# A mixing projection as seven products of quarters, with the second norm's operands through DRAM and three heads at the MLP's start

## The chip, the cores and the metric

The kernel runs on one core of one Trainium2 chip. The metric is the device time of one execution in microseconds (us); the median of three runs of the kernel before is 2449.32 us (2448.23 to 2449.37). The engines are TensorE (PE; its weight loads stand as PEld), VectorE (DVE), ScalarE (ACT), GpSimd (POOL) and SyncE (SP). POOL and SP issue the DMAs here, each from a queue of its own that works in order.

## The reference

One layer on 512 tokens of width 2048, float32 in and out. What matters here is the second half:

```python
conv_branch = jnp.einsum('bsc,cd->bsd', conv_y, w_conv_out[l])      # 1024 -> 2048
attn_branch = jnp.einsum('bsc,cd->bsd', attn, w_attn_out[l])        # 1024 -> 2048
merged = gc * conv_branch + ga * attn_branch
x = x + jnp.einsum('bsd,de->bse', merged, w_mix_out[l])             # 2048 -> 2048
h = rmsnorm(x, g_mlp[l])
u = jnp.square(jax.nn.relu(jnp.einsum('bsd,df->bsf', h, w_ff1[l]))) # 2048 -> 8192
x = x + jnp.einsum('bsf,fd->bsd', u, w_ff2[l])
return rmsnorm(x, g_final)
```

`gc` and `ga` are sigmoid gates. `rmsnorm` divides each row by the root of its mean square and multiplies by a gain per column.

## The kernel before

**Arithmetic.** Every float32 operand of a matmul is split into a high part in the matmul's format and the rest (`split`, L101 on ScalarE and L102 on VectorE), and each product is made of three matmuls: high times high, low times high, high times low.

**Seven products.** Most projections are made in groups of 512 output columns by a scheme of seven products of quarters instead of eight. Rows (256 tokens each) and columns (256 each) are halved, the inner dimension is halved into even and odd blocks of 128. The activations' quarters A11, A12, A21, A22 give seven operands: A11, A12, A22 themselves, S1 = A21 + A22, S3 = A11 - A21, S2 = S1 - A11, S4 = A12 - S2. The weights' quarters X[i, j] are loaded one by one (1 MB each, `Group.load`, on SP's queue, into four slots x0 to x3) and combined by VectorE in place (L105). `Group.head` makes the products A11 and A12 from X[0, 0] and X[1, 0]; `Group.tail` makes S4, S2, S3, S1 and A22, `Group.tail2` S1, S3, S2, S4 and A22 in that order. In `tail`, S4 takes X[1, 1] as it is, and S2 and S3 take differences with it. Each product is 48 matmuls of 256 columns. The banks that collect them are called a, b, c and d; ScalarE's snapshots (L207) and VectorE's additions (L108) combine them, and a `put` takes each finished quarter (i, j). The split halves th and tl have two buffers each. A `Group` may carry an extra matmul of 192 columns ahead of a product (L138) or beside it (L712).

**Order.** The program is traced in order and a planner then arranges each engine's instructions by their program order and by when it reckons them ready. A tile is named by its tag; a tag has the number of buffers given, most have one, and a new tile of a tag waits for the last use of the old one. Between PE's stages there is no barrier.

**The stages around the change.**

- `conv_out(c)` (L818): the conv projection for 512 columns as seven products of half size (24 matmuls each), with weights in three slots, two tiles per group. `put` (L832) multiplies by the gates and leaves the quarter in `held`, in slot x1; for c = 3 it goes to DRAM (`held_d`, L834). The gates come by POOL's queue (L824).
- `attn_out(c)`: the attention projection as an ordinary sum over eight blocks (`gemm_t`, L347 to L349, 96 matmuls of 512 columns). For each of four banks, VectorE multiplies by the gate (L847) and adds `held` (L108), and the sum is split into the operand M of the mixing (eight splits of 256 columns). The attention operands themselves stand in t3 and t2. The order is conv 0, attention 0, conv 1, attention 1, conv 2, conv 3, attention 2, attention 3.
- The mixing (`gemm_n`, L354 to L356): M is stationary, 512 weight columns move; 16 blocks of the inner dimension, four row tiles, four column blocks, three matmuls each. The weights come in 24 loads of 1 MB (L326), since column blocks 2 and 3 are passed over twice, for two row tiles each time. `add_into` adds x, sums squares on ScalarE (L380) and writes the new rows to DRAM (L898).
- The class `Blocks`: while later blocks of the mixing run, finished rows are transposed on TensorE (L935, 64 in all), multiplied by the gain (L943), and the seven operands of the MLP are made from them and stay in SBUF.
- The MLP's first half: 16 groups `ff1(g)` of 512 columns. Group 0 is `head(True, rest)`, `Q2.sums(3)` and `tail2`, where `rest` turns the last rows and computes the rows' factors; groups 1 to 15 are `head` and `tail`. `put_u` squares the quarters, makes the seven operands of the second half's left side (the two `sums`, L1041, L1057, L1058) and writes them to DRAM (L1060, L1061). Groups 1 to 15 carry the extra matmul beside S2 (L712). The fourth weight slot of group 0 is x1, which before it held rows of the mixing (`rows_block`).
- The MLP's second half follows and is not touched.

## Time and profile before

| what | value |
| --- | --- |
| median of three runs | 2449.32 us |
| profiled execution, first to last instruction | 2450.8 us (the profile gives no other time of it) |
| mean granted TensorE clock | 0.999 |
| TensorE busy / weight loads | 2423.2 us / 2252.6 us |
| VectorE, ScalarE, GpSimd busy | 1970.8, 1180.1, 230.3 us |
| first conv group starts, first mixing matmul, first MLP matmul | 864.75, 1031.4, 1211.8 us |
| second half of the MLP starts | 1830.2 us |

A row of a table of stretches gives the stretch, its length, and for each engine the busy us and the number of instructions (x), then the granted clock, the share of DMA time and GB/s. A row of the timeline gives start, duration, engine, line, operation, output <- inputs, and in brackets how long the engine was idle before and what ended that. A row of groups gives line, engine, operation, tiles, shapes, count, then busy us and mean ns of one, then idle time before and what ended it. Matmul ends are modelled and overlap: the time between starts tells the pace.

### The profile page before, as it was taken

Reading aid. Unit: us, or ns where it says so; the run is one execution under the profiler, and the core shown is the slowest. Engines: PE = TensorE matmul, PEld = TensorE weight load, DVE = VectorE, ACT = ScalarE, POOL = GpSimd, SP = SyncE. Lnnn points to the kernel's source line nnn. Section 1 sums busy time; section 2 is a strip of 40 time slices with the busy share of each in tenths; the row PEclk is TensorE's granted clock in tenths of the full one; section 3 lists DMA queues with packets and bytes.
Section 4 is the critical chain, followed back from the end, with each engine's and each line's share of the span. In section 5 each row is a group of like instructions: output and inputs, shape, how many; then the busy total and the mean of one; then the engine's idle time right before and its main releaser. Section 6 shows DMA issues by size and latency. Waiting matters only on the chain.

```text
span 2450.8 us, 40086 instructions
## 1 busy us (share of the span) xinstructions
PE 2423.2 (99%) x17224; PEld 2252.6 (92%) x17224; DVE 1970.8 (80%) x1665; ACT 1180.1 (48%) x1189; POOL 230.3 (9%) x369
## 2 busy tenths in 40 slices
PE   8999999999999999999999999999999999999998
PEld 8999899999999999888899999999998888888886
DVE  7987777788887777535688898888988888889898
ACT  6443434345455544335555666666655333333334
POOL 0100000111121110000000000000011001100000
PEclk9999999999999999999999999999999999999999
DMA  7664544454656654635645646656588566655662
GB/s 250 183 192 142 154 133 146 138 160 165 211 172 214 215 186 155 216 114 205 199 169 185 231 173 216 216 202 228 177 302 293 168 247 227 237 191 183 244 225 101
DMA packets 276597, 475.62 MB, mean 194 GB/s; under 512 B 10732, under 2 KB 180836, under 8 KB 276036
## 3 DMA queue, kind: packets, MB, share of 16 engines
q1 hardware_dynamic: 232592, 291.59, 37.0%
q0 software_dynamic: 42960, 180.38, 19.8%
q8 instruction: 135, 2.21, 0.4%
q10 hardware_dynamic: 868, 1.10, 0.1%
q14 instruction: 42, 0.34, 0.0%
HBM read 374.46 MB, written 98.57 MB: 193 GB/s over the span
## 4 chain that ended last, share of the span: by engine, by line
PE 93%; DVE 3%; DMA 1%; issue 1%; ACT 1%; POOL 0%; SPq 0%; DVEq 0%; POOLq 0%; ACTq 0%
PE a L145 6%; PE a L147 6%; PE a L149 6%; PE d L149 5%; PE d L145 5%; PE d L147 5%; PE a L163 5%; PE a L165 5%; PE a L162 5%; PE c L145 4%; PE c L147 4%; PE c L149 4%; PE b L145 3%; PE b L147 3%; PE b L149 3%; PE d L165 3%
## 5 line engine op out<-in xcount | busy, mean ns | idle before, releaser
L101 ACT ACTIVATE th<-x 128x2048 fp32r<-128x2048 f32 (+1 forms) x252 | 483.4, 1918 | 462.3 <-DVE x L105 153.8
L102 DVE TENSOR_TENSOR tl<-x,th 128x2048 fp32r<-128x2048 f32 (+1 forms) x252 | 575.1, 2287 | 159.0 <-ACT th L101 144.1
L105 DVE TENSOR_TENSOR x<-x,x 128x2048 f32<-128x2048 f32 (+1 forms) x144 | 329.2, 2286 | 19.9 <-DMA x<-in_w_in_dram 16.2
L101 ACT ACTIVATE th<-y 128x2048 fp32r<-128x2048 f32 (+1 forms) x109 | 184.8, 1700 | 268.8 <-PE a L163 138.8
L102 DVE TENSOR_TENSOR tl<-y,th 128x2048 fp32r<-128x2048 f32 (+1 forms) x109 | 218.9, 2013 | 30.0 <-ACT th L101 29.5
L162 PE MATMUL a<-th,us 128*128 128x512 f32 x512 | 199.2, 389 | 0.0
L163 PE MATMUL a<-th,us 128*128 128x512 f32 x512 | 199.2, 389 | 0.0
L145 PE MATMUL a<-ST,th 128*128 128x256 f32 x752 | 174.1, 277 | 0.6 <-ACT th L101 0.6
L147 PE MATMUL a<-ST,th 128*128 128x256 f32 x752 | 173.6, 277 | 0.0
L102 DVE TENSOR_TENSOR tl<-raw,th 128x2048 fp32r<-128x2048 f32 x32 | 73.4, 2292 | 101.8 <-ACT th L101 101.5
L145 PEld LDWEIGHTS a<-ST,th 128*128 128x128 f32 x752 | 141.3, 188 | 0.9 <-ACT th L101 0.8
L147 PEld LDWEIGHTS a<-ST,th 128*128 128x128 f32 x752 | 141.3, 188 | 0.0
L165 PE MATMUL a<-tl,us 128*128 128x512 f32 x512 | 136.8, 389 | 0.0
L145 PE MATMUL c<-S,th 128*128 128x256 f32 x576 | 134.2, 278 | 0.0
L147 PE MATMUL c<-S,th 128*128 128x256 f32 x576 | 133.8, 277 | 0.0
L101 ACT ACTIVATE th<-t 128x2048 fp32r<-128x2048 f32 x31 | 59.5, 1920 | 126.1 <-DVE t L105 73.0
L145 PE MATMUL d<-ST,th 128*128 128x256 f32 x512 | 118.2, 277 | 0.0
L147 PE MATMUL d<-ST,th 128*128 128x256 f32 x512 | 118.2, 277 | 0.0
L162 PEld LDWEIGHTS a<-th,us 128*128 128x128 f32 x512 | 96.1, 188 | 20.0
L165 PEld LDWEIGHTS a<-tl,us 128*128 128x128 f32 x512 | 96.0, 188 | 20.1 <-DVE tl L102 0.2
L163 PEld LDWEIGHTS a<-th,us 128*128 128x128 f32 x512 | 96.1, 188 | 19.9
L101 ACT ACTIVATE th<-raw 128x2048 fp32r<-128x2048 f32 x32 | 61.4, 1919 | 103.0 <-PE pn L356 42.7
(362 smaller groups left out, 6517.3 us busy)
## 6 DMA issues: line engine op xcount, KB each, us to landing
x<-in_w_in_dram SPq DMA_DIRECT2D x86, 1024.0 KB, 5.9
x<-in_w_ff_dram SPq DMA_DIRECT2D x64, 1024.0 KB, 8.4
y<-in_w_ff_dram SPq DMA_DIRECT2D x64, 1024.0 KB, 8.4
us<-s_d POOLq DMA_DIRECT2D x48, 1024.0 KB, 9.2
s_d<-rh POOLq DMA_DIRECT2D x32, 896.0 KB, 5.5
s_d<-r POOLq DMA_DIRECT2D x32, 896.0 KB, 5.5
raw<-in_w_mix_out_dram SPq DMA_DIRECT2D x24, 1024.0 KB, 5.2
g_d<-o POOLq DMA_DIRECT2D x32, 256.0 KB, 3.1
```

Of the source, the lines that this page charges most:

```text
L101: nc.scalar.activation(out=hi, in_=src, func=AF.Copy, scale=one)
L102: nc.vector.tensor_tensor(out=lo, in0=src, in1=hi.bitcast(F32), op=ALU.subtract)
L105: nc.vector.tensor_tensor(out=out, in0=a, in1=b, op=ALU.subtract)
L145: nc.tensor.matmul(o, hi[:, q, js], Sh, start=first and q == 0 and j == 0, stop=False, skip_group_check=True)
L147: nc.tensor.matmul(o, hi[:, q, js], Sl, start=False, stop=False, skip_group_check=True)
L149: nc.tensor.matmul(o, lo[:, q, js], Sh, start=False, stop=q == nq - 1, skip_group_check=True)
L162: nc.tensor.matmul(o, Sh, hi[:, q, :], start=begin and q == 0, stop=False, skip_group_check=True)
L163: nc.tensor.matmul(o, Sl, hi[:, q, :], start=False, stop=False, skip_group_check=True)
L165: nc.tensor.matmul(o, Sh, lo[:, q, :], start=False, stop=q == nq - 1, skip_group_check=True)
```

## The change

The mixing becomes four `Group`s of 512 columns with seven products each; M is stationary, the weights move, 256 columns at a time. Its seven operands are made in the attention projection, by `Products.quads` after each `attn_out(c)`, on quarters of 128x512. To have room, all four conv groups run first and write their gated quarters to DRAM, and each attention projection loads them into x1 and adds into them there; x1 is split after that. The operands of c = 3 go to t2 and t3 once the attention operands are done with.

`Mix.put` takes a finished quarter of the mixing: adds x, sums squares, writes rows, transposes (four a quarter) and multiplies by the gain. The seven operands of the MLP are written to DRAM (`f_d`) by three of the four groups, loaded again whole during the last (`begin_part`), split there or behind the MLP's heads (`split_part`), and completed by the last group's part directly.

The MLP begins with the heads of groups 0, 1 and 2, and their tails (`tail2`) follow; the first quarter of each is squared at once and kept in DRAM (`hu_d`). Their weight quarters X[0, 0] and X[1, 0] are loaded twice. Groups 3 to 15 stay as they were. The extra matmuls of groups 0 to 2 become one ahead of S3.

```diff
+    class Products:                       # at[n, c]: [P, high/low, 2, HS]
+        def place(self, k, units):
+            self.tile(main.tile([P, 4, 2, 2, HS], F32R, tag=f"t{k}", name="M"), units)
+        def quads(self, c, t):
+            (a11, a21), (a12, a22) = ([t[:, par, h] for h in range(2)] for par in range(2))
+            def put(n, src):
+                split(src, self.at[n, c][:, 0], self.at[n, c][:, 1])
+            put("A11", a11)
+            put("A12", a12)
+            put("A22", a22)
+            add(a22, a21, a22)
+            put("S1", a22)
+            sub(a21, a11, a21)
+            put("S3", a21)
+            sub(a11, a22, a11)
+            put("S2", a11)
+            sub(a12, a12, a11)
+            put("S4", a12)
...
-            o = v if far else held[c][:, 2 * j:2 * j + 2, ts]
-            nc.vector.tensor_tensor(out=o, in0=v, in1=gates[i, j], op=ALU.mult)
-            if far:
-                nc.gpsimd.dma_start(out=held_d[2 * j:2 * j + 2, :, ts].rearrange("k p s -> p k s"), in_=o)
+            nc.vector.tensor_tensor(out=v, in0=v, in1=gates[i, j], op=ALU.mult)
+            nc.gpsimd.dma_start(out=held_d[c, 2 * j:2 * j + 2, :, ts].rearrange("k p s -> p k s"), in_=v)
...
     def attn_out(c, banks):
+        t = main.tile([P, 2, 2, 2, HS], F32, tag="x1", name="merged")
+        for j in range(4):
+            nc.gpsimd.dma_start(out=t[:, j % 2, :, j // 2, :], in_=held_d[c, j].rearrange("p (h s) -> p h s", h=2))
...
-            add(g, g, held[:, j, :])
-            k = 4 * c + j
-            for p in range(2):
-                hi, lo = M[p, k // 8]
-                split(g[:, p * HS:(p + 1) * HS], hi[:, k % 8, :], lo[:, k % 8, :])
+            o = t[:, j % 2, :, j // 2, :]
+            add(o, g.rearrange("p (h s) -> p h s", h=2), o)
         gemm_t(w_attn_out, CT, c * S, aact, banks, cons_at)
+        if c == 3:
+            M.place(2, [(n, 3) for n in ("A11", "A12", "S4", "S2")])
+            M.place(3, [(n, 3) for n in ("S3", "S1", "A22")])
+        M.quads(c, t)
...
+    for c in range(4):
+        conv_out(c, (lower, upper)[c % 2])
...
+    for c in range(4):
+        attn_out(c, (lower, upper)[c % 2])
+    n = turns[0] + 1
+    free[:] = [cycle[(n + i) % 3] for i in range(3)] + [1]
...
+    def begin_part(n, k):
+        Q2[n] = pair(k, F32R, n).rearrange("p e (q s) -> p e q s", q=KT // 2)
+        nc.gpsimd.dma_start(out=Q2[n][:, 1, :KT // 2 - 2].bitcast(F32), in_=f_d[:, PARTS.index(n)])
+    def split_part(n):
+        lo = Q2[n][:, 1, :KT // 2 - 2]
+        split(lo.bitcast(F32), Q2[n][:, 0, :KT // 2 - 2], lo)
+    class Mix:
...
+        def put(self, i, j, v):
+            add(v, v, self.x.pop((i, j)))
+            for t in range(2):
+                square_part(v[:, t, :], ss2[:, 2 * i + t, 2 * g + j:2 * g + j + 1], bank(4, "junk")[:, :HS])
+            nc.gpsimd.dma_start(out=x1_d[2 * i:2 * i + 2, :, c:c + HS].rearrange("t p c -> p t c"), in_=v)
+            pt = bank(5 + (2 * i + j) % 3, "ptr").rearrange("p (two s) -> p two s", two=2)
+            for par in range(2):
+                for t in range(2):
+                    nc.tensor.transpose(pt[:, par, t * P:(t + 1) * P], v[:, t, par * P:(par + 1) * P], ident)
+            for par in range(2):
+                nc.scalar.activation(out=self.F[i][:, par, j, :], in_=pt[:, par, :], func=AF.Copy,
+                                     scale=gmlpT[:, k + par:k + par + 1])
...
+        def out(self, n, src):
+            if self.last:
+                split(src, Q2[n][:, 0, 2 * g:], Q2[n][:, 1, 2 * g:])
+            else:
+                nc.gpsimd.dma_start(out=f_d[:, PARTS.index(n), 2 * g:2 * g + 2], in_=src)
...
+    for g in range(4):
+        mix = Mix(g)
+        after = {"S3": mix.fourth}
...
+        group = Group(w_mix_out, g * S, g * S + HS, HS, M.moving, mm_rows, steady(g), mix.put, after=after)
+        group.head(True, before)
+        group.tail()
+        before = mix.sums
...
+    heads = [ff1(g, ((a,), (3,), (1,), (7,))) for g, a in enumerate((5, 0, 2))]
+    heads[0].head(False, rest)
+    behind_heads("S1")
+    heads[1].head(False, lambda: behind_heads("S3"))
+    behind_heads("S2")
+    heads[2].head(False, lambda: behind_heads("S4"))
+    behind_heads("A22")
...
+    for g in heads:
+        g.tail2()
...
-    for g in range(1, DFF // S):
+    for g in range(AHEAD, DFF // S):
```

`Mix.sums` makes S1, S3, S2 and S4 of a group from its four gained quarters, as `quads` does; `fourth` loads the last rows of x of a group behind S3; `behind_heads` splits the loaded part of an operand and then the last group's part of it.

More of the change, by code (lines that the diff above doesn't have):

```diff
@@ L1014, in tile_hybrid_block, with after_s4, after_s2 @@
[L1014 removed]
+            self.parts = {"S1": s1, "S3": a21, "S2": a11, "S4": a12, "A22": a22}
+            if not self.last:
+                for n, src in self.parts.items():
+                    self.out(n, src)
+    before = lambda: None
+    for g in range(4):
+        mix = Mix(g)
+        after = {"S3": mix.fourth}
+        if g == 3:
+            def after_s4():
+                begin_part("A12", 6)
+                split_part("A11")
+            def after_s2():
+                begin_part("S1", 0)
+                begin_part("S3", 2)
+                split_part("A12")
+            after.update({"A12": lambda: begin_part("A11", 4), "S4": after_s4, "S2": after_s2,
+                          "S1": lambda: begin_part("S2", 1)})
+        group = Group(w_mix_out, g * S, g * S + HS, HS, M.moving, mm_rows, steady(g), mix.put, after=after)
+        group.head(True, before)
+        group.tail()
+        before = mix.sums
```

220 lines of the change are left out of this document (74 added, 146 removed).

## The prediction

> **What bounds the kernel now.** I read the page's busy times and chain first, then a table of stages, then single waits.
>
> ```profile
> PE 2423.2 (99%) x17224; PEld 2252.6 (92%) x17224; DVE 1970.8 (80%) x1665; ACT 1180.1 (48%) x1189; POOL 230.3 (9%) x369
> PE 93%; DVE 3%; DMA 1%; issue 1%; ACT 1%; POOL 0%; SPq 0%; DVEq 0%; POOLq 0%; ACTq 0%
> ```
>
> TensorE carries 93% of the chain that ended last. Less TensorE work is a gain wherever VectorE, next at 80%, and the loads keep up. The table shows where they do (busy us and instructions of each engine in a stretch).
>
> ```profile
> core 0: us, PE busy (x) PEld busy (x) DVE busy (x) ACT busy (x) POOL busy (x), PEclk, DMA share, GB/s
> 1036.00:1080.00 44.00, 44.00 (x196) 36.44 (x195) 12.15 (x9) 10.46 (x12) 1.46 (x2) 1.00 0.40 138
> 1320.00:1820.00 500.00, 500.00 (x4414) 500.00 (x4413) 438.27 (x328) 314.02 (x314) 30.05 (x56) 1.00 0.60 211
> 1274.00:1310.00 36.00, 36.00 (x308) 36.00 (x307) 29.67 (x22) 20.36 (x20) 2.13 (x4) 1.00 0.63 219
> 864.75:884.02 19.27, 19.27 (x173) 19.27 (x171) 15.82 (x16) 9.86 (x12) 5.55 (x8) 1.00 0.67 219
> 947.54:966.83 19.29, 19.29 (x171) 19.28 (x170) 17.44 (x22) 10.68 (x15) 1.45 (x2) 1.00 0.30 95
> 966.83:987.51 20.68, 20.06 (x172) 19.75 (x171) 17.65 (x19) 9.40 (x11) 2.91 (x4) 1.00 0.47 160
> 884.02:906.15 22.13, 22.11 (x98) 17.94 (x97) 14.29 (x20) 4.95 (x8) 1.45 (x2) 1.00 0.59 208
> 1226.00:1236.00 10.00, 8.75 (x76) 8.56 (x75) 7.93 (x6) 3.42 (x4) 0.00 (x0) 1.00 0.00 0
> 1236.00:1240.00 4.00, 3.37 (x29) 3.17 (x28) 3.97 (x3) 3.76 (x3) 0.00 (x0) 1.00 0.61 183
> ```
>
> The first row is the mixing projection: less the two matmuls that its edges cut, one of 512 columns every 0.2268 us. The next two are the MLP's first half: one of 256 columns every 0.1133 us for 500 us, but every 0.1176 us in the stretch before it, at the same granted clock. So a half-length matmul costs half, and there are two paces 4.3 ns apart. The slow one stands behind the waits of the last two rows (1.25 and 0.63 us). The four middle rows are conv 0, conv 2, conv 3 and one attention projection: conv 3, which alone follows another conv directly, takes 20.68 instead of 19.28 us.
>
> **Part 1, seven products.** Lines 354 to 356 issue 16 x 4 x 4 x 3 = 768 matmuls of 512 columns: 174.2 us. After: 4 groups x 7 products x 2 blocks x 8 x 3 = 1344 of 256: 152.3 us. Gain 21.9. The transposes are 64 on both sides. All of it is on TensorE's path. At the slow pace it would be 5.8 less (1344 x 4.3 ns); every wait and each of the 16 sets of transposes may change the pace, so I take half: +2.9, ends 0 and 5.8.
>
> On the fixed cost of a matmul the Trainium skill ("TensorE: Matmul & The Clock Gate", section "Wait — 56ns, not 53.3ns?") says otherwise than these rows: N / 2.4 GHz plus about 2.5 ns each. By it the count of 1344 against 768 would pay, and the gain be an estimated 18.9 us; the trace has 0.2268 = 2 x 0.1134, so the measurement decides.
>
> VectorE in a mixing group:
>
> ```profile
> L102 DVE TENSOR_TENSOR tl<-x,th 128x2048 fp32r<-128x2048 f32 (+1 forms) x252 | 575.1, 2287 | 159.0 <-ACT th L101 144.1 <-PE a L149 9.5 <-ACT p L640 4.7
> L101 ACT ACTIVATE th<-x 128x2048 fp32r<-128x2048 f32 (+1 forms) x252 | 483.4, 1918 | 462.3 <-DVE x L105 153.8
> L207 ACT ACTIVATE o<-a 128x512 f32<-128x512 f32 x93 | 54.3, 584 | 5.3 <-PE a L149 5.3
> L1058 DVE TENSOR_TENSOR r<-r,rh 128x1792 f32<-128x1792 f32 x32 | 64.6, 2018 | 1.8 <-ACT rh L1057 1.8
> L105 DVE TENSOR_TENSOR r<-r 128x256 f32<-128x256 f32 x64 | 26.8, 419 | 0.5
> 1225.40 0.68 DVE L108 TENSOR_TENSOR o<-b,o 128x512 f32<-128x512 f32 x1
> 1226.00 0.68 DVE L102 TENSOR_TENSOR ST<-up,ST 128x512 fp32r<-128x512 f32 x1
> raw<-in_w_mix_out_dram SPq DMA_DIRECT2D x24, 1024.0 KB, 5.2
> ```
>
> Back to back they overlap by 0.08 (1225.40, then 1226.00), so count 2.2, 1.9, 0.6 and 0.34. Seven splits and four differences are 11 x 2.2 = 24.2, twelve evictions, additions and sums 12 x 0.6 = 7.2: 31.4 of 38.1 us of TensorE. The MLP stretch runs without a wait at 438.27 / 500 = 88%, so at 82% this is covered. ScalarE, 314 of 500 us there, has seven splits of 1.9 and some 20 steps of at most 0.6, 25 us: covered too. The loads of this stage shrink from 24 of 1 MB to 16.
>
> **Part 2, four convs in a row, then four attention projections.** Conv 1, 2 and 3 now each follow a conv; before it was one.
>
> ```profile
> 968.42 1.23 DVE L105 TENSOR_TENSOR y<-y,y 128x1024 f32<-128x1024 f32 x1 [1.37 <-DMA y<-in_w_conv_out_dram]
> 990.43 1.45 POOL L834 DMA_DIRECT2D held_d<-o  x2 [4.61 <-DVE o L832]
> ```
>
> The first row is conv 3's first difference, waiting for a weight tile whose slot the previous conv gave back late; VectorE, with 17.4 us of work in 19.3, doesn't catch up. Two more such convs by that row are 2 x 1.4 = 2.8, and nothing if the planner loads earlier: I take 2.0. On POOL's queue held_d grows from 4 writes to 16, with 16 loads back: 28 more issues of 0.73 us over 170 us, on an engine 9% busy: 0 (if it held up the gates' loads behind it, up to 1). An attention projection's VectorE work rises from 14.3 by 11 x 0.6 less 8 x 0.34 to 18.2 of 22.1: covered, and so are x1's loads for the next c, which wait for its quads.
>
> **Part 3, the handover from attention to mixing.** The first group's fourth weight quarter goes to slot x1, and x1 holds the merged values of attention 3 until the last of their seven splits. Its operands for c = 3 go to t2 and t3, which hold the attention operands until the last matmul. The same slot was late before at the MLP's start:
>
> ```profile
> 1218.55 0.37 SPq L190 DMA_DIRECT2D x<-in_w_ff_dram  x1
> 1227.20 2.28 DVE L105 TENSOR_TENSOR x<-x,x 128x2048 f32<-128x2048 f32 x1
> 1229.58 1.91 ACT L101 ACTIVATE th<-x 128x2048 fp32r<-128x2048 f32 x1 [2.01 <-DVE x L105]
> 1231.55 0.35 PE L138 MATMUL d<-ST,th 128*128 128x192 f32 x1 [1.25 <-ACT th L101]
> 1238.20 0.38 PE L145 MATMUL a<-ST,th 128*128 128x256 f32 x1 [0.63 <-ACT th L101]
> ```
>
> From the last attention matmul: two operations on bank 3, four sums and seven splits, 13 x 0.6 = 7.8, with one 2.2 split of A12's weights between them: 8 to 10 until x1 is free; load 5.2, ScalarE split 1.9: S4 can start at 15 to 17. A11 and A12 last 2 x 48 x 0.1133, so TensorE asks at 11: a wait of 6, and about 1 for the differences behind it, as at 1238.20. Ends: 2.7 (no weight split between, every ScalarE step hidden) and 9. A11's own c = 3 part waits for t2: 0.6 + 0.6 after the last matmul against 12 matmuls x 0.113 = 1.4: +0.5 (0 to 1.5). Behind S4 wait S2, S3 and, in a's order, S1; X10's and X01's loads are not behind it on SP.
>
> Such a pause is longer than any within the run. What the clock does then:
>
> ```profile
> 8.58 6.03 PE L414 MATMUL ptr<-dg,xn 128*128 128x128 f32 x32 [1.97 <-DMA bf<-in_b_f_dram]
> 14.87 1.38 PE L414 MATMUL ptr<-dg,xn 128*128 128x128 f32 x10 [0.26 <-ACT dg L496]
> 2441.30:2443.50 2.20, 0.00 (x0) 0.00 (x0) 1.43 (x3) 1.41 (x4) 0.00 (x0) 1.00 0.57 213
> 2443.50:2450.80 7.30, 0.00 (x0) 0.00 (x0) 1.57 (x3) 1.33 (x2) 0.55 (x1) 0.50 0.63 223
> ```
>
> At the start, from no matmuls, 32 take 6.03 us, 0.19 each; soon after, ten take 1.38, 0.14 each with a small wait: 32 x 0.05 = 1.6 lost, and more without that wait. At the end the granted clock is 0.50 from 2.2 us after the last matmul's modelled end. So after 6 us without one I expect half speed for a while and take the start's loss: +2.0 (0 if the wait stays below 2.2). The Trainium skill ("TensorE: Matmul & The Clock Gate", "Part 1: The HAM clock gate (the "warmup" mystery)") speaks against the change here: half clock after an idle window of about 3.4 us, full again after about 3.4 us of work. By it this would cost an estimated 1.7; the trace agrees in direction.
>
> **Part 4, second norm through DRAM, last mixing group to MLP.** Group 3's (0,1) quarter must reach A11's last two rows: from the end of S1 a snapshot, four VectorE steps, eight short ScalarE steps, 13 x 0.6 = 7.8 at most; needed after A22 and 24 matmuls more, (48 + 24) x 0.1133 = 8.2. So 0, ends 0 and 3. POOL gains 21 writes and 7 loads of f_d, 8 and 8 of rows: 44 x 0.73 = 32 us over 190: covered; each part is read half a group or more after its last write.
>
> **Part 5, three heads, three tails.**
>
> ```profile
> 1219.02 0.39 PE L1024 MATMUL mean<-ms,ones 128*128 128x4 f32 x2 [0.31 <-ACT down L943]
> L145 PE MATMUL a<-ST,th 128*128 128x256 f32 x752 | 174.1, 277 | 0.6 <-ACT th L101 0.6
> ```
>
> The waits at 1219, 1231 and 1238 go: 0.31 + 1.25 + 0.63, and 3 x (0.277 - 0.113), by which a matmul's modelled end lies behind the next start: -2.7. What is late next is VectorE. A tail has 5 splits and 4 differences, 9 x 2.2 = 19.8, evictions 2.4, and the two sums 2 x (4 x 0.34 + 1.95) = 6.6: 28.8 in 5 x 5.44 = 27.2 us of TensorE. The heads (6 x 5.44 = 32.6) have six splits and three evictions, 15, five parts of 1.65 + 0.6 (three quarters of a split and a short one), 11, and the last mixing group's additions and sums, 8 x 0.6: 31. The first tail has no sums of a group before it. Together 31 + 86.4 - 3.3 = 114.1 against 114.2: no slack, so I take +3 (0 to 8). The quarters that the heads load again (6 more MB over 114 us) and hu_d's six transfers are covered by the DMA share of 0.60.
>
> **Sum.** -21.9 + 2.9 + 2.0 + 7.0 + 2.0 + 0.5 - 2.7 + 3.0 = -7.2 us, to 2443.6 in the profiled execution, whose span of 2450.8 is 1.5 above the median of the runs, 2449.32. From the median: 2442.1.
>
> **Rivals.** (a) The handover hides: x1 comes free early and the tails hold. Pace +1, wait 2.7, the old waits gone: -21.9 + 1 + 2.7 - 2.7 = -20.9, 2428.4. For it: 1320 to 1820 shows four-quarter groups without a wait. Against: x1 has one buffer. (b) VectorE holds the tails: +9 instead of 3 (each of 15 products 0.6 late, the length of an eviction): 2448.1, no change. For it 28.8 against 27.2; against it that sums can slip into group 3's slack of 12%. (c) Slower: the transposes. Before, they read rows that were finished one chunk, 10.9 us, earlier; now they are issued directly behind the product that makes their rows. If they stand there in TensorE's order, each set waits for two VectorE steps:
>
> ```profile
> 953.39 0.69 DVE L108 TENSOR_TENSOR o<-b,o 128x512 f32<-128x512 f32 x1 [0.64 <-PE b L149]
> ```
>
> A matmul's 0.28 and twice 0.69 are 1.65, 16 of them 26: 2468. From 8 of the 16 standing so (12.1 / 1.65) the kernel is slower. Against: in the attention stage the planner put dependent matmuls between others, and PE still has 99%. (d) Not doing what it says is excluded: the loops fix the counts. The fixed cost per matmul of the Trainium skill ("TensorE: Matmul & The Clock Gate", the section named above) would give 3 us more, 2445; the rows leave it no chance.
>
> **Chances.** Forecast 0.50 (its own range 2435 to 2450), (a) 0.15, (b) 0.15, (c) 0.20. Within 0.2% is 2444.4 to 2454.2, about what a measurement of this kernel can tell from no change. The forecast gives faster 0.37, same 0.12, slower 0.01; (a) faster 0.15; (b) 0.03, 0.07, 0.05; (c) same 0.02, slower 0.18. Together faster 0.55, same 0.21, slower 0.24. The range reaches to (a) and into (c): 2428 to 2461.
>
> **What would show it.** Right: 1344 matmuls of 256 columns at 0.113 to 0.118; one wait of 5 to 9 us before S4 of the first mixing group, ended by ScalarE's split behind a DMA into x1, and a granted clock of 0.50 behind it; VectorE above 95% in the tails; two more convs of 20 to 21 us. Wrong: TensorE idle in front of each set of transposes; the first mixing group running through; waits in the attention stage for x1's loads.

## The result, and the profile after

The changed kernel takes 2484.61 us (median of four runs, 2480.06 to 2488.80), the kernel before 2448.89 (four runs beside them). The ratio is 1.0145, 95% interval 1.0128 to 1.0162: slower, where 2442.1 was forecast with a range up to 2461. The profiled execution is one of the longer ones, with a span of 2487.1 us against 2450.8.

```profile
PE 2423.0 (97%) x17799; PEld 2276.9 (92%) x17799; DVE 2041.4 (82%) x1699; ACT 1201.7 (48%) x1218; POOL 281.3 (11%) x447
```

TensorE is busy for as long as before (2423.2) in a span 36 us longer, although 21.9 us of its matmuls are gone: the loss is idle time and slower matmuls. Until the last matmul, the clock's records show 0.50 granted (a half clock, below) for 30.7 us in the changed kernel and never in the kernel before; and the mixing runs at the slow pace, 117.8 instead of 113.3 ns a matmul. (Line numbers are the changed kernel's, two or three higher than before in the code that both share.) By stage (columns as in the prediction's table of stretches), first the kernel before, then the changed one; the rows are convs with attention, mixing, the MLP's first half, its second half:

```profile
864.75:1031.36 166.61, 165.94 (x1066) 149.46 (x1065) 122.04 (x147) 63.29 (x83) 15.70 (x22) 1.00 0.53 179
1031.36:1211.80 180.44, 180.44 (x826) 149.95 (x825) 89.70 (x82) 79.98 (x109) 10.94 (x15) 1.00 0.53 178
1211.80:1830.21 618.41, 616.22 (x5404) 615.62 (x5403) 537.50 (x406) 384.04 (x390) 39.34 (x70) 1.00 0.59 205
1830.21:2440.90 610.69, 610.04 (x2691) 504.21 (x2689) 532.75 (x395) 239.98 (x170) 55.13 (x74) 1.00 0.61 214
```

```profile
866.78:1040.81 174.03, 168.46 (x1066) 151.14 (x1065) 136.15 (x152) 65.57 (x74) 37.47 (x52) 1.00 0.64 205
1040.81:1222.45 181.64, 170.83 (x1402) 168.56 (x1400) 138.50 (x103) 96.70 (x141) 34.95 (x55) 0.98 0.61 194
1222.45:1854.80 632.35, 620.20 (x5403) 618.59 (x5403) 542.75 (x412) 384.16 (x391) 45.74 (x80) 0.99 0.61 215
1854.80:2477.50 622.70, 612.64 (x2690) 505.10 (x2688) 534.93 (x397) 242.09 (x173) 53.94 (x72) 0.99 0.60 208
```

The stages differ by +7.4, +1.2, +13.9 and +12.0 us; 2.0 more are lost ahead of the first conv, in unchanged code, where a half clock of 3.41 us follows a wait of TensorE in this execution; it comes in some executions and not in others (last section) and is not the change's. Foreseen were +2.0, -9.5, +0.3 and nothing. The second half of the MLP, which the change does not touch, has lost almost as much as any. Where TensorE stood, place by place:

**The second half's start.** Two kinds of loads are issued around it: the second half's first operands us on POOL's queue, and its first weights y on SP's. Rows of POOL's issues, and the row of the four y loads (KB each, median us from issue to landing), first before (y from 1800 to 1832 us), then after (1820 to 1850 us):

```profile
1804.02 1.54 POOL L1109 DMA_DIRECT2D us<-s_d  x2
1824.88 3.01 POOL L1109 DMA_DIRECT2D us<-s_d  x4 [5.46 <-PE a L149]
y<-in_w_ff_dram SPq DMA_DIRECT2D x4, 1024.0 KB, 12.1
```

```profile
1833.42 2.25 POOL L1112 DMA_DIRECT2D us<-s_d  x3 [4.11 <-PE c L151]
y<-in_w_ff_dram SPq DMA_DIRECT2D x4, 1024.0 KB, 22.4
```

And the timeline of the changed kernel there:

```profile
1865.81 2.29 DVE L107 TENSOR_TENSOR y<-y,y 128x2048 f32<-128x2048 f32 x1 [9.91 <-DMA y<-in_w_ff_dram]
1871.89 1.65 PE L167 MATMUL b<-tl,us 128*128 128x512 f32 x3 [8.21 <-DVE tl L104]
```

The weight loads y are the same and issued equally early, the first 19.9 us before the second half begins (at 1810.43 and 1834.95). Before, two of the eight us loads go ahead of it and the next four come 14.5 us behind it; in the changed kernel five go ahead, the last three of them directly before it. The y loads then take 22.4 us instead of 12.1. VectorE's first difference waits 9.9 us for one, the rest of A12's split is queued behind it, and TensorE waits 8.2 for that, with a half clock of 6.83 us from 1868.78.

**The tails of the three heads.**

```profile
1298.84 0.54 POOL L1054 DMA_DIRECT2D s_d<-r  x1 [2.54 <-DVE r L1051]
1308.73 0.55 POOL L1037 DMA_DIRECT2D r<-hu_d  x1 [9.35 <-DMA s_d<-r]
1308.53 0.42 ACT L1032 ACTIVATE r<-o 128x256 f32<-128x256 f32 x1 [7.44 <-DMA s_d<-r]
1316.43 0.58 PE L147 MATMUL c<-S,th 128*128 128x256 f32 x1 [4.48 <-ACT o L210]
1349.71 0.43 DVE L107 TENSOR_TENSOR r<-r,o 128x256 f32<-128x256 f32 x1 [4.61 <-DMA r<-hu_d]
```

Tile r has one buffer. The reload of a head's first quarter goes straight into it, so it starts only when the write of r's last content to DRAM has landed, 9.6 us after its issue (1298.84 to 1308.4). ScalarE stands in its queue until then, VectorE until the reload itself has landed (the last row is the second time), and the snapshot of bank c, which the next tail's first product needs, stands behind them. It happens three times; the writes take 9.6, 10.0 and 3.9 us. During the first two the DMA share is 0.97 and 1.04.

**The handover from attention to mixing.** The load into x1, its split, the first matmul of S4; then the stretch of S4's product, with its clock:

```profile
1052.23 0.38 SPq L192 DMA_DIRECT2D x<-in_w_mix_out_dram  x1
1058.49 1.91 ACT L103 ACTIVATE th<-x 128x2048 fp32r<-128x2048 f32 x1 [0.98 <-DMA x<-in_w_mix_out_dram]
1060.45 0.58 PE L164 MATMUL c<-th,M 128*128 128x256 f32 x1 [4.04 <-ACT th L103]
```

```profile
1060.45:1068.98 8.53, 8.53 (x48) 8.53 (x49) 8.46 (x5) 2.60 (x2) 0.00 (x0) 0.64 0.00 1
```

**The convs and the last mixing group.** The first two rows are conv 1, the others the last transposes that precede group 3's end:

```profile
889.47 1.23 DVE L107 TENSOR_TENSOR y<-y,y 128x1024 f32<-128x1024 f32 x1 [2.77 <-DMA y<-in_w_conv_out_dram]
892.48 0.62 PE L151 MATMUL b<-ys,tl 128*128 128x256 f32 x3 [1.03 <-DVE tl L104]
...
1216.17 2.29 DVE L104 TENSOR_TENSOR tl<-x,th 128x2048 fp32r<-128x2048 f32 x1
1218.38 0.68 DVE L110 TENSOR_TENSOR o<-o 128x512 f32<-128x512 f32 x1
1219.10 0.69 DVE L110 TENSOR_TENSOR o<-o,xr 128x512 f32<-128x512 f32 x1
1219.93 0.80 PE L950 MATMUL ptr<-ident,o 128*128 128x128 f32 x4 [2.28 <-DVE o L110]
```

**The pace.** One product of 48 matmuls in the mixing and one in the heads:

```profile
1080.29:1085.94 5.65, 5.65 (x50) 5.65 (x49) 2.29 (x1) 2.40 (x3) 0.00 (x0) 1.00 0.76 209
1235.28:1240.72 5.44, 5.44 (x51) 5.44 (x49) 5.44 (x6) 5.44 (x7) 0.62 (x1) 1.00 0.42 117
```

At a granted clock of 1.00 both, 117.8 and 113.3 ns a matmul. All of the mixing runs at the slow one here.

### The profile page after: what moved, and what is told of

It reads as the page before. It is cut to its first block, busy times and chain, and to the rows that moved or that the text cites. A ratio compares the mean times of both kernels' runs of the same rounds, so it can differ in the third digit from the quotient of the medians.

```text
span 2487.1 us, 41509 instructions
## 1 busy us (share of the span) xinstructions
PE 2423.0 (97%) x17799; PEld 2276.9 (92%) x17799; DVE 2041.4 (82%) x1699; ACT 1201.7 (48%) x1218; POOL 281.3 (11%) x447
## 3 DMA queue, kind: packets, MB, share of 16 engines
q0 software_dynamic: 48624, 200.30, 21.9%
q8 instruction: 139, 2.28, 0.4%
## 5 line engine op out<-in xcount | busy, mean ns | idle before, releaser
L104 DVE TENSOR_TENSOR tl<-x,th 128x2048 fp32r<-128x2048 f32 (+1 forms) x280 | 639.6, 2289 | 178.0 <-ACT th L103 162.8
L103 ACT ACTIVATE th<-x 128x2048 fp32r<-128x2048 f32 (+1 forms) x280 | 537.0, 1918 | 513.2 <-DVE x L107 157.9
L107 DVE TENSOR_TENSOR x<-x,x 128x2048 f32<-128x2048 f32 (+1 forms) x160 | 366.1, 2288 | 28.3 <-DMA x<-in_w_in_dram 15.7
L147 PE MATMUL c<-S,th 128*128 128x256 f32 x880 | 206.8, 280 | 6.0 <-ACT o L210 4.5
L149 PE MATMUL c<-S,th 128*128 128x256 f32 x880 | 206.1, 279 | 0.0
L147 PE MATMUL a<-S,th 128*128 128x256 f32 x752 | 176.5, 280 | 0.3 <-ACT o L210 0.3
L149 PE MATMUL a<-S,th 128*128 128x256 f32 x752 | 175.1, 278 | 0.0
L147 PEld LDWEIGHTS c<-S,th 128*128 128x128 f32 x880 | 167.4, 190 | 6.7 <-ACT o L210 4.7
L149 PEld LDWEIGHTS c<-S,th 128*128 128x128 f32 x880 | 167.3, 190 | 0.0
L147 PEld LDWEIGHTS a<-S,th 128*128 128x128 f32 x752 | 142.4, 189 | 0.5 <-ACT o L210 0.5
L149 PEld LDWEIGHTS a<-S,th 128*128 128x128 f32 x752 | 142.4, 189 | 0.0
L147 PE MATMUL a<-A,th 128*128 128x256 f32 x544 | 127.2, 279 | 0.8 <-ACT th L103 0.8
L147 PE MATMUL b<-A,th 128*128 128x256 f32 x544 | 126.7, 278 | 0.1
L149 PE MATMUL a<-A,th 128*128 128x256 f32 x544 | 126.7, 278 | 0.0
L149 PE MATMUL b<-A,th 128*128 128x256 f32 x544 | 126.5, 277 | 0.0
L147 PE MATMUL d<-S,th 128*128 128x256 f32 x544 | 126.4, 278 | 0.0
L149 PE MATMUL d<-S,th 128*128 128x256 f32 x544 | 125.8, 277 | 0.0
```

The lines of the kernel that those rows point to most:

```text
L103: nc.scalar.activation(out=hi, in_=src, func=AF.Copy, scale=one)
L104: nc.vector.tensor_tensor(out=lo, in0=src, in1=hi.bitcast(F32), op=ALU.subtract)
L107: nc.vector.tensor_tensor(out=out, in0=a, in1=b, op=ALU.subtract)
L147: nc.tensor.matmul(o, hi[:, q, js], Sh, start=first and q == 0 and j == 0, stop=False, skip_group_check=True)
L149: nc.tensor.matmul(o, hi[:, q, js], Sl, start=False, stop=False, skip_group_check=True)
```

## The experiments

Each edit is made on the changed kernel, or from the eighth on, on a run named there. Times are medians with the ratio to the kernel before in the same series; what two runs differ by within a stage comes from their profiles.

**1. The second half's first loads.** A22 to t5, so that this slot comes free last.

```diff
-    begin_part("S4", 5)
-    begin_part("A22", 3)
+    begin_part("S4", 3)
+    begin_part("A22", 5)
```

> Edit: the MLP's operands S4 and A22 change places (S4 in t3, A22 in t5), nothing else. Theory: in the changed kernel five of the eight loads of the second half's first operands (us) are issued 32 to 20 us before the second half begins, ahead of its four weight loads (y), because t5, t6 and t2 come free early; the y loads then take 22 to 25 us instead of 9 to 13, VectorE waits 9.9 us for one, and TensorE 8.6 us behind VectorE. With A22 in t5, that slot comes free with the last product, and the loads queued behind it on POOL go late as well: the wait of 8.6, the one of 1.5 and the half clock behind them go, about 11 us, 2473.5 us. Rival: the y loads are late because their own slots are given back in another order than before; then nothing changes, 2484.

Measured 2476.69, ratio 1.0112 (1.0097 to 1.0127); the second half takes 616.1 us instead of 622.7. Fewer of the us loads go ahead of the weights, which then land earlier, and the wait shrinks from 8.2 to 3.1:

```profile
y<-in_w_ff_dram SPq DMA_DIRECT2D x4, 1024.0 KB, 18.6
```

```profile
1864.86 1.65 PE L167 MATMUL b<-tl,us 128*128 128x512 f32 x3 [3.06 <-DVE tl L104]
```

Four of the eight are still issued before the first weight load, those into t4 and t6; the planner put them ahead of the ones that wait for t5. The rest of this loss goes in run 8, where they are held back by a dependency.

**2. Four conv slots.**

```diff
+    ring, taken = [cycle[0], 1, cycle[1], cycle[2]], [0]
-                self.at[i, j] = main.tile([P, 2, self.nq, self.w], F32, tag=f"x{slot()}", name=f"y{j}")
+                self.at[i, j] = main.tile([P, 2, self.nq, self.w], F32, tag=f"x{ring[taken[0] % 4]}", name=f"y{j}")
+                taken[0] += 1
```

> Edit: the eight weight tiles of the four conv projections go round four slots (x1 with them) instead of three. Theory: the seven waits of TensorE in the convs (0.8 to 1.6 us, 7.5 together) come from weight tiles whose slot the conv before gives back late; with a fourth slot they are loaded a tile earlier and the waits go: 7 us less, 2477.5, and the four convs take 78 to 80 us instead of 86.8. Rival: VectorE's work at 17.5 of 19.3 us, with held and gates on top, is what lags; then the convs stay at 85 us or more and the time at 2483 to 2485.

Measured 2482.41, ratio 1.0133 (1.0118 to 1.0148). All seven waits are gone, and a new one has come in conv 0, with a half clock behind it:

```profile
866.24 1.23 DVE L107 TENSOR_TENSOR y<-y,y 128x1024 f32<-128x1024 f32 x1 [5.67 <-DMA y<-in_w_conv_out_dram]
871.55 0.55 PE L147 MATMUL b<-ys,th 128*128 128x256 f32 x1 [4.63 <-DVE o L110]
```

Slot x1 comes free later than the others, and as the second of the round it held up conv 0's own second tile. So the mechanism holds and the edit was a bad one; run 6 puts x1 last.

**3. The heads' first quarters loaded ahead.**

```diff
-            if j == 0 and g < AHEAD:
-                nc.gpsimd.dma_start(out=r[:, 0:2], in_=hu_d[g])
-            elif j == 0:
+            if j == 0:
...
-    for g in heads:
+    for n, g in enumerate(heads):
+        c = pf.tile([P, 2, HS], F32, tag="c", name="c")
+        nc.gpsimd.dma_start(out=c, in_=hu_d[n])
+        held.append(c)
         g.tail2()
```

> Edit: the squared first quarter of each of the three heads (hu_d) is loaded into a buffer of its own ahead of its tail and copied from there by ScalarE, as in the later groups, instead of being loaded into r itself. Theory: r has one buffer; the load into it starts only when the write of the last r has landed, 8 to 10 us after its issue, and takes 3 to 5.6 us more, and VectorE's and ScalarE's queues stand behind it three times (at 1309, 1344 and 1377 us): TensorE's waits of 4.8 us in the third tail and of 8.7 us in group 3 and two half clocks follow. With the load out of this chain most of 13 us goes: 2473 to 2476. Rival: VectorE has simply more work than TensorE in three tails and the wait only shows where it runs out of slack; then less than 4 us go, 2481 or more.

Measured 2476.14, ratio 1.0106 (1.0089 to 1.0123): 8.5 us less. The two profiled executions differ by 11.7, of which the MLP's first half, the one stage that the edit touches, gives 5.7 (632.4 to 626.6): between the theory's most of 13 and the rival's less than 4. VectorE's stops for r<-hu_d are gone. ScalarE still stands for the write of r (first row), and what is left of the third tail's wait is 2.7 us, still ended by the snapshot of bank c, which all three tails shared (second row). Behind that tail VectorE is busy without a pause (third row), and TensorE waits 0.7, 0.6 and 2.0 us there for splits. So the reload was one cause; VectorE, the rival, which has no slack to catch up, has a part in what is left:

```profile
1304.32 0.63 ACT L1037 ACTIVATE r<-c 128x512 f32<-128x512 f32 x1 [7.55 <-DMA s_d<-r]
1310.77 0.58 PE L147 MATMUL c<-S,th 128*128 128x256 f32 x1 [2.71 <-ACT o L210]
1339.00:1366.00 27.00, 23.68 (x185) 22.99 (x185) 27.00 (x23) 18.96 (x20) 2.35 (x5) 0.94 0.44 170
```

**4. X[1, 1] ahead of X[0, 1].**

```diff
-            X = self.quarters((0, 1), (1, 1))
+            X = self.quarters((1, 1), (0, 1))
```

> Edit: in the order of the second two weight quarters of a group, X[1, 1] is loaded before X[0, 1]; so in the first mixing group X[0, 1], not X[1, 1], goes to x1. Theory: TensorE's wait of 4.3 us before S4 of the first mixing group, and the half clock behind it (S4's product takes 8.5 us instead of 5.65), come from x1, which holds the merged values until the last of their splits. X[0, 1] is needed one product later (for S2's difference), so the wait shrinks to 1 us or less and the half clock goes: 6 us less, 2478.5. Rival: VectorE's queue (seven splits and four sums of the merged values between the weight splits) is what S4 waits for; then the wait stays at 3 us or more, 2483 or more.

Measured 2488.65, ratio 1.0159 (1.0144 to 1.0174): a miss. S4 has no wait, and S2 waits instead, longer:

```profile
1060.69 9.27 DVE L107 TENSOR_TENSOR x<-x,x 128x2048 f32<-128x2048 f32 x4 [5.60 <-DMA x<-in_w_mix_out_dram]
1069.63 0.58 PE L164 MATMUL a<-th,M 128*128 128x256 f32 x1 [9.94 <-ACT th L103]
```

All of VectorE's differences begin from X[0, 1]; whichever quarter is in x1, S2 cannot start before that slot's load has come: 29.8 us after the mixing's start here (1039.87 to 1069.63), 28.2 in the changed kernel (1040.81 to 1068.98).

**5. The last merged values apart from x1.**

```diff
-        t = main.tile([P, 2, 2, 2, HS], F32, tag="x1", name="merged")
+        if c < 3:
+            both = main.tile([P, 2, 2, 2, HS], F32, tag="x1", name="merged")
+            t = [both[:, par] for par in range(2)]
+        else:
+            t = [pm.tile([P, 2, 2, HS], F32, tag=f"f{i}", name="merged") for i in range(2)]
```

> Edit: the merged values of the last attention projection stand in the two tiles that later hold the mixing's gained quarters (f0, f1) instead of x1; so x1 is free for a weight quarter of the first mixing group one attention projection earlier. The run before this one showed that loading X[1, 1] ahead of X[0, 1] only moved the wait from S4 to S2 (10.2 us), where the differences need both. Theory: the landing of the quarter in x1 decides, and x1 is held by the merged values. Then the wait before S4 (4.1 to 4.3 us) and the half clock behind it (S4's product 8.5 instead of 5.65) go: 6.5 us less, 2478. Rival: VectorE's and ScalarE's queues of splits decide; then S4 or S2 still waits 3 us or more, 2483.

Measured 2474.8, ratio 1.0101 (1.0086 to 1.0116). Behind waits of 0.4 and 1.5 us for the operands of c = 3, which stay, the first group's products follow one another, at full clock; the mixing takes 6.7 us less:

```profile
1036.19:1211.13 174.94, 167.14 (x1402) 164.72 (x1400) 136.37 (x104) 95.86 (x141) 34.95 (x55) 1.00 0.60 195
```

Slot x1 was the handover's cost. The time fell by 9.8, of which the stage explains 6.7; the convs were 1.7 shorter and the start 2.9, which the edit does not touch.

**6. Four conv slots, x1 last.**

```diff
-    ring, taken = [cycle[0], 1, cycle[1], cycle[2]], [0]
+    ring, taken = cycle + [1], [0]
```

> Edit: as with the four slots for the conv weights before, but x1 comes last in the round, not second. With x1 second the seven waits inside the convs went (one of 0.8 to 1.6 us each), but conv 0's second tile was loaded 5 us later, since x1 came free late, and TensorE waited 4.9 us for it at the first product but one and fell to half clock. Theory: the late slot is the whole of the convs' loss; with x1 last both go: the four convs take 77 to 80 us instead of 86.8 and the time is 2476 to 2478. Rival: the load of the fourth tile, now early, delays what the first conv needs: a wait of 3 us or more in conv 0 stays, 2481 or more.

Measured 2473.26, ratio 1.0096 (1.0081 to 1.0111). The four convs in the changed kernel and here:

```profile
866.78:953.60 86.82, 81.25 (x683) 79.15 (x682) 71.53 (x76) 37.60 (x45) 25.90 (x36) 1.00 0.65 210
```

```profile
864.69:943.62 78.93, 77.84 (x683) 77.46 (x681) 70.94 (x76) 38.38 (x46) 25.82 (x36) 1.00 0.65 219
```

7.9 us less for the same work of VectorE: it was the slot, not the work.

**7. One head.** `AHEAD = 1`, and one entry in `heads`.

```diff
-    heads[0].head(False, rest)
-    behind_heads("S1")
-    heads[1].head(False, lambda: behind_heads("S3"))
-    behind_heads("S2")
-    heads[2].head(False, lambda: behind_heads("S4"))
-    behind_heads("A22")
+    heads[0].head(False, rest)
+    behind_heads("S1", "S3", "S2", "S4", "A22")
```

> Edit: the MLP begins with one head instead of three (AHEAD = 1), its five parts are split behind that head, and its tail follows; groups 1 to 15 run as groups 3 to 15 did. Theory: the three heads bring more waiting than they save, by the reload of the first quarter through r (13 us of waits and half clocks at 1311 to 1386 us); with one head TensorE waits for the parts' splits, five of 2.4 us in 10.9 us of products, 2 to 5 us, and the reload happens once: 2475 to 2480. Rival: the heads are needed to cover the parts; then the tail of group 0 waits 8 us or more and falls to half clock, 2485 or more.

Measured 2478.25, ratio 1.0111 (1.0093 to 1.013): 6.4 less. The MLP's first half falls to 620.7, and the mixing's end, where splits now crowd, gives back 2.8 of it:

```profile
1222.50:1843.20 620.70, 616.09 (x5404) 615.49 (x5403) 540.09 (x410) 383.80 (x396) 44.78 (x76) 0.99 0.60 209
```

**8. Five edits together:** runs 3, 5 and 6, other banks c and d for the second head, and a copy ahead of three of the second half's first operand tiles that waits for the last group's S1 quarter (`mark`).

```diff
-    heads = [ff1(g, ((a,), (3,), (1,), (7,))) for g, a in enumerate((5, 0, 2))]
+    heads = [ff1(g, ((a,), (3,), (c,), (d,))) for g, (a, c, d) in enumerate(((5, 1, 7), (0, 4, 6), (2, 1, 7)))]
...
+            if seg == 0 and k > 0:
+                nc.gpsimd.tensor_copy(t[:, :, 0, 0, 0:1], mark)
```

> Edits together: the merged values of the last attention projection apart from x1; four conv slots with x1 last; the heads' first quarters loaded ahead into a buffer of their own; the heads' banks c and d alternating with two free banks; and the loads of three of the second half's first four operand tiles held back until S1's quarter of the last MLP group is there. If the waits are separate losses, the gains add: 6.5 + 7.5 + 8.5 + 2 + 11 = 35 us, 2449, level with the kernel before; what is left of the change's 21.9 us is then the slow pace (6), group 3's end (5.5) and single waits. If the waits are one shortage of VectorE or of DMA that moves on to the next place when a wait is taken out, less than half of this comes: 2467 or more.

Measured 2448.21 (ten runs), ratio 0.9994 (0.9985 to 1.0003): 36.4 less than the changed kernel, where 35 was expected if the gains add. So the losses were separate in the main. Runs 3, 5 and 6 had shown three of the five edits alone; the other banks and the held-back loads were not run alone.

```profile
865.93:1031.61 165.68, 165.00 (x1067) 149.26 (x1065) 136.20 (x151) 65.65 (x74) 37.36 (x52) 1.00 0.65 218
1031.61:1204.34 172.73, 166.42 (x1401) 164.08 (x1400) 136.41 (x104) 95.68 (x141) 35.05 (x55) 1.00 0.61 197
1204.34:1827.42 623.08, 618.01 (x5402) 616.85 (x5403) 546.09 (x416) 388.01 (x399) 41.99 (x75) 1.00 0.62 216
1827.42:2437.00 609.58, 609.54 (x2689) 504.11 (x2688) 531.49 (x394) 239.67 (x170) 58.66 (x81) 1.00 0.60 215
```

The second half is back to 609.6; the mixing is 7.7 below the kernel before, the MLP's first half still 4.7 above it.

**9. Extra matmuls against the slow pace,** on run 8.

```diff
+        if extra:
+            nc.tensor.matmul(ps[0][:, :192], Sx(0)[0][:, :P], hi[:, 0, :192], start=True, stop=False,
+                             skip_group_check=True)
...
+                      extra={"A12": "first", "S3": "first"})
```

> Edit on the run with the five edits together: an extra matmul of 192 columns ahead of A12 and S3 in each mixing group, and ahead of A12 in the MLP's heads (12 matmuls of about 0.09 us; their sums are overwritten). There the mixing's products still take 5.65 us for 48 matmuls (117.8 ns each), as in the changed kernel, and the heads and first tail too, against 5.44 (113.3 ns) elsewhere, at a granted clock of 1.00 in both. Theory: the pace is a state of TensorE's stream that an odd matmul sets to the fast one, as the rows behind the extra matmuls of the convs and of the MLP show; then 28 x 0.21 = 6 us in the mixing and 2.4 in the heads go, less 1.1 for the extras: 2441. Rival: the slow pace belongs to the mixing's operands (row blocks of 128 stationary, weights moving) or to its transposes, and comes back behind each; then the mixing stays at 5.65 us and the time at 2447 to 2449.

Measured 2453.7, ratio 1.0011 (1.0002 to 1.0020): a miss. Behind each of the eight extra matmuls the mixing's product is as slow as ever (49 matmuls, first row), and the stage takes 175.3 us instead of 172.7. What the expectation starts from does not hold throughout, though: in run 8 itself, without extra matmuls, two stretches of the mixing run at the fast pace, each between two sets of transposes. In one of them 96 matmuls start in 10.88 us (second row, which counts two more that its edges cut):

```profile
1059.35:1065.11 5.76, 5.76 (x51) 5.76 (x50) 2.29 (x1) 2.39 (x3) 0.00 (x0) 1.00 0.92 276
1121.00:1131.88 10.88, 10.88 (x98) 10.88 (x97) 10.88 (x9) 5.97 (x11) 5.15 (x9) 1.00 0.64 217
```

**10 to 12, on run 9.** Run 10 begins S3's and S2's loads later (`begin_part("S3", 2)` behind S1, `begin_part("S2", 1)` behind the group), run 11 has one head, run 12 two.

> Edit on the run before this one: the loads of the operands S3 and S2 of the MLP from DRAM (and with them their splits) begin one and two products later in the last mixing group. Theory: the waits at that group's end (2.6 us at the transposes, 0.9 and, in the changed kernel, 1.3) come from splits of operands that the planner put ahead of the weight splits and additions on ScalarE and VectorE; fewer of them there take 2 to 3 us off. Rival: the splits only move into the heads, which have no slack on VectorE (31 of 32.6 us), and TensorE waits there instead: no gain or a loss up to 3.

> Edit on the run with the extra matmuls: one head instead of three. In the changed kernel one head took 11.6 us off the MLP's first half and put 2.8 on the mixing, but there the reload of the heads' first quarters through r still cost 13. With that reload repaired, theory: three heads and one head are about level, the tails behind three heads still waiting 5.4 us (2.3, 0.7, 2.4) where one head waits 5.4 (3.3, 1.1, 1.1) and falls to half clock once: within 3 us of the run before. Rival: three heads in a row cost VectorE what it does not have, whatever the reload; then one head is 4 us or more faster.

> Edit on the run with the extra matmuls: two heads instead of three. Theory: with two, the parts' splits are covered nearly as well, and one tail less follows without its head between; 1 to 4 us faster than three. Rival: the waits come from r's single buffer and sit in the tails whatever their number; then level within 1 us.

Measured 2452.94 (1.0008; 0.9999 to 1.0017), 2451.75 (1.0005; 0.9996 to 1.0014) and 2447.15 (0.9985; 0.9976 to 0.9994). In run 10 the waits at group 3's end only changed places (3.2 and 0.7 us instead of 0.6 and 2.3). One head is level with three once the reload is repaired, and two are 6.5 better: the first half takes 618.2 us with two, 621.3 with one, 625.1 with three.

**13. Two heads without the mixing's extra matmuls,** on run 8 (`AHEAD = 2`).

> Edit on the run with the five edits together: two heads instead of three, and an extra matmul ahead of A12 in the heads alone (none in the mixing, where eight of them left the pace as it was and the stage 2.6 us longer). Theory: two heads are worth 3 to 6 us (the run with two heads and the extra matmuls was 6.5 below the one with three) and the mixing's extra matmuls cost 1 to 2: 2442 to 2446, faster than the kernel before by 0.2 to 0.3%. Rival: the difference of two heads lies within what the pauses and half clocks of a run vary by: 2448 or more.

Measured 2444.57 (eleven runs, 2441.99 to 2447.71), ratio 0.9979 (0.9971 to 0.9988): faster than the kernel before by 0.2%, and the best here. Mixing and first half:

```profile
1030.61:1203.94 173.33, 167.42 (x1402) 165.19 (x1401) 137.17 (x105) 96.35 (x141) 34.84 (x55) 0.99 0.62 198
1203.94:1822.82 618.88, 616.44 (x5406) 615.84 (x5405) 544.69 (x413) 387.54 (x399) 41.10 (x73) 1.00 0.60 213
```

**14. Without transposes,** on run 8; ScalarE reads the rows themselves.

```diff
-                    nc.tensor.transpose(pt[:, par, t * P:(t + 1) * P], v[:, t, par * P:(par + 1) * P], ident)
...
-                nc.scalar.activation(out=self.F[i][:, par, j, :], in_=pt[:, par, :], func=AF.Copy,
+                nc.scalar.activation(out=self.F[i][:, par, j, :], in_=v[:, par, :], func=AF.Copy,
```

> Edit on the run with the five edits together: the 64 transposes of the mixing are left out, and ScalarE makes the gained quarters from the rows as they are; so the values from the second norm on are not the reference's, while every other instruction stays. The mixing takes 172.7 us with the transposes: 152.3 at the fast pace, 6 for the slow one, 5.8 for 16 sets of 0.36, the rest waits. Theory A: the transposes bring the slow pace; then the mixing's products take 5.44 us and the stage 157 to 160 us. Theory B: the slow pace stays without them; then the products take 5.65 and the stage 162 to 166, and the transposes are worth their own 5.8 and the waits of 4 us in front of them.

Measured 2452.52, ratio 1.0011 (1.0001 to 1.0020). Three products in a row still take 5.65 each:

```profile
1056.58:1073.54 16.96, 16.96 (x146) 16.96 (x145) 9.03 (x5) 7.19 (x7) 0.00 (x0) 1.00 0.70 210
```

So the slow pace needs no transposes. Their price stays open: the stage takes 170.95 us, not 162 to 166, since new waits of 0.8 to 3.1 us came in other places of the reordered queues.

**15. All three reloads begun behind the last group,** on run 13.

> Edit on the first run of this call (two heads): the loads of the operands S1, S3 and S2 from DRAM begin behind the last mixing group, not in it. Theory: the two waits at that group's end (1 us for a weight split behind an operand's split on ScalarE, 2.6 at the transposes behind VectorE's operand splits) go, 3 to 5 us with the half clock behind them, and the heads and tails give back up to 3, since the splits move there: 0 to 4 us faster than the first run of this call. Rival: with two heads there is no room for them; the first tail waits for S1 or S3 5 us or more, and the run is slower than the first.

Measured 2445.79, ratio 0.9982 (0.9974 to 0.9991): level with run 13. The edit did not do what it should: the planner issued these three reloads at 1183.9, 1186.7 and 1194.8 us, where run 13, whose mixing begins 1.3 us earlier, has 1182.7, 1184.8 and 1193.5, and their splits (S<-S) stand where they stood:

```profile
1197.22 1.76 DVE L104 TENSOR_TENSOR S<-S 128x1536 fp32r<-128x1536 f32 x1 [0.21 <-ACT S L103]
1199.03 2.29 DVE L104 TENSOR_TENSOR tl<-x,th 128x2048 fp32r<-128x2048 f32 x1
1201.24 0.69 DVE L110 TENSOR_TENSOR o<-o 128x512 f32<-128x512 f32 x1
```

Whether these splits cause the wait at the last transposes was therefore not told apart. What is seen is VectorE in order: a split, a weight split, and only then the addition that the transposes wait for.

## Why the prediction was wrong

Of the 43.5 us between the forecast of -7.2 and the +36.3 of the two profiled executions, 10.7 lie in the mixing, 5.4 in the convs, 13.6 in the MLP's first half, 12.0 in its second half, 2.0 at the start; the end is 0.3 shorter.

- **Failed: Part 5, "the quarters that the heads load again ... and hu_d's six transfers are covered by the DMA share of 0.60".** The share was right as a mean (0.61) and says nothing of one transfer or of order: it was 0.97 and 1.04 while the reload waited for writes of 9.6 and 10.0 us out of the same buffer, and three engines' queues stood behind it. Run 3 takes 5.7 us away by moving the reload, run 8 with other banks 9.3. VectorE's load, which the step was about, was 85% in the first tail (23.2 of the 27.2 us from 1257.0 to 1284.2), not above 95%: the changed kernel's tails were held by waits. Rival (b), VectorE's work, does not fall with that. Once the reload was moved, VectorE had no pause for 27 us behind the third tail (run 3); how much of the 4.7 us that run 8 leaves is its work was not separated.
- **Failed by omission: the sum has no term for the second half.** I took "not touched" for "not affected". The new places of the MLP's operands free t5, t6 and t2 earlier, loads start earlier and collide with the weights. Run 1 shows the direction, run 8, together with its other edits, all 13 us (622.7 to 609.6).
- **Failed in size: Part 2, "two more such convs by that row are 2 x 1.4".** The stage lost 7.4. The mechanism was the one named, a slot given back late (run 6 takes it away), but conv 3 before had landed its tile in 5.4 us and these took 6.4 to 7.3 beside the gates and held_d, and each conv stops TensorE at two or three places, where the forecast had one wait.
- **Right in its mechanism: Part 3.** 7 + 2 + 0.5 was forecast for the handover; measured are waits of 4.0 and 1.5 around the first transposes, 8.53 - 5.65 = 2.9 for the half clock, and some 1.8 in A11 and A12 for the c = 3 part. Run 5 takes 6.7 away by freeing x1. That the sum is so near, 9.5 against 10.2, is partly luck: the working's 15 to 17 less 11 gives a wait of 4 to 6, of which it took the 6, and the 1.8 lies beyond the upper end of 1.5.
- **Part 1's gain is there, its two reserves were too small.** The slow pace took its upper end, 6 us (28 products x 0.21), not half. Of rival (c) two places in sixteen came true, 1.5 us in group 0 and 2.3 in group 3, with a half clock (the same waits stand in Parts 3 and 4).
- **Part 4, 0 with ends 0 and 3:** measured some 1.2, 2.3 and a half clock of 1.0, all VectorE's and ScalarE's order at the last group's end. What exactly sets that order is open (runs 10 and 15).

With these losses repaired (run 13) the mixing is 7.1 us shorter than before (180.4 to 173.3). Of the 14.8 that are missing from the 21.9, the pace takes 5.2 (two stretches run at the fast one, as in run 8); waits of 1.7 and 0.6 at the start, 0.6 twice at transposes and 2.4 at the end, with a half clock of about 1.0 behind the last, take 6.9; 2.7 are spread over the edges of products and transposes.

## What to carry to other kernels

Ask of every transfer that is moved or added which buffer it writes, what must have landed before, and which in-order queues stand behind it; the mean DMA share answers none of these. When an operand moves to another slot, follow that slot to its next user, even in a stage that the change does not touch: a load that starts earlier can take its time from the one that is needed first. And when several waits are found, repair them one by one and then together; here five repairs, three of them also made alone, brought back what had been lost.

## What the runs showed of the hardware

Half clocks come in spans of 3.41, 6.83 or 10.24 us. In the sixteen profiles of the changed kernel and its variants, between the first 100 us and the last matmul, all 20 waits of TensorE (idle time before a matmul) over 3.1 us are overlapped by one or followed by one within 1.6 us, 21 of the 29 between 2.2 and 3.1, and 6 of the 17 between 1.9 and 2.2. The length alone does not decide: the same wait of 2.27 or 2.28 us, at about 21 us in code that no edit touches, goes with a half clock in 7 of all 17 profiles and not in the other 10. The first conv starts at 865.8 to 866.9 us in the seven and at 863.8 to 864.8 in the ten. The Trainium skill ("TensorE: Matmul & The Clock Gate", "Part 1: The HAM clock gate (the "warmup" mystery)") names a free-running window of 3413 ns, and the spans agree with it; it asks for a whole idle window, and here waits from 1.94 us on were sometimes enough.

The two paces, 113.3 and 117.8 ns for 256 columns at a full granted clock, last for hundreds of matmuls, in one kernel and on the same line of code. An extra matmul is followed by the fast one in some places (in the kernel before at 1311.9 us, in run 9's heads at 1238.1) and by the slow one in others (at 1272.2 and 1226.7 in the same two, and eight times in run 9's mixing). Transposes are not needed for the slow one (run 14), but the pace can change at them: in run 8 it turns fast behind those that end at 1120.8 us and slow again behind those at 1132.8. What sets it is open, and it is worth 4%.
